# A hybrid RWKV-7, Mamba-2 and MoE block: order of the triangular inverses, place of the b and k transposes, rows of the rest weights

## The chip, the cores and the metric

One core of a Trainium2 chip runs the whole kernel in one launch. The metric is the device time in microseconds. Engines: TensorE (PE), VectorE (DVE), ScalarE (ACT), GpSimd (POOL), and SyncE (SP), which issues most of the transfers.

## The reference

One layer on 512 latent and 256 context tokens, D = 1024: adaLN modulation, a mixer of two branches (RWKV-7 in both directions, Mamba-2 SSD in both directions), a gated merge, then 16 expert-choice experts. The change touches the RWKV branch alone. Its preparation and its recurrence for each of 16 heads and both directions are:

```python
w_raw = rw_w0 + einsum('blde,def->bldf', tanh(xw), rw_w2)   # low-rank, 64 columns per direction
decay = exp(-exp(-softplus(-w_raw) - 0.5))
a = sigmoid(rw_a0 + einsum('blde,def->bldf', xa, rw_a2))
kk = l2norm(k * rw_kk);  k_eff = k * (1 + (a - 1) * rw_ka)
sa = einsum('bhvk,bhk->bhv', s, -kk_t)
s = s * w_t + sa * (kk_t * a_t) + v_t * k_t
y = einsum('bhvk,bhk->bhv', s, r_t)
```

## The kernel before

The kernel has stages: norms and adaLN (to about 110 us), the RWKV pair stage (about 110 to 690), the RWKV chunk scan (about 680 to 870), the SSD scan, the merge and the experts. The recurrence is computed in chunks of 64 tokens, 12 per direction; within a chunk the products of the scaled vectors form triangular matrices, whose inverses the scan needs.

`rw_all` runs the pair stage: eight pairs of heads, p = 0 to 7, direction d = 0 and 1 in each. Per pair: `rw_elem(p, 1)` prepares the other direction's vectors (two calls of `low()`, each two matmuls for 512 latent and two for 256 context tokens: one with `lwh`, the rounded weights, on 128 rows, and one with `lwl`, the rest weights, on the direction's 64 rows); `rw_products(p, 0)`; the bonus (`rw_bonus`); `rw_head` and `rw_elem(p + 1, 0)` for the next pair; `rw_products(p, 1)`; and `tri(p)`.

`rw_products` stores AR, multiplies BK by AR in three groups (tile `pab`, with `TENSOR_TENSOR` into X by DVE after each), stores X to DRAM, and then transposes BK in three groups of four chunks (`pbt`, copied to BT by ACT and stored to BTd by ACT's queue). A call f() after each piece pushes about 2600 columns of the input projection (`pl`, `pc`) into PE's order as fill; in the last pairs, when all inputs are projected, 1500.

`tri(p)` inverts the 16x16 and 32x32 blocks of the stored products on DVE, step by step. It loads them as Ad (three transfers), works on T, on the scratch tile W and on Tf, ends with the copy Tt<-Tf and stores Tf and Tt to DRAM. `tri2(p)` loads them back (TT in four transfers, T11 in two, A21 in two), and makes two small products on PE, `px` and `py` (32x32), and stores TT for the scan. `tri2(p - 2)` is a generator t2 that `rw_products` steps: once after each of two X tiles' stores, once after each of three `pbt` groups. tri(7) and the last two tri2 run in `rw_last`, beside the scan.

PE's order is the order in which the code is written. DVE, ACT, POOL and SP run in an order that a scheduler works out when the kernel is built, from the order written and its own estimates. Each engine then runs its instructions in order. The PSUM pool `ra` has four buffers of one tag, shared by `low()`, `pab`, `pbt`, `px`, `py`, `pvt` and `pb`.

Of the kernel before, what the change touches and what calls it, by code (L numbers as in the profile page):

```python
# [42 lines left out]
TL = 7  # L43
# [28 lines left out]
RHT = 1500  # L72
# [15 lines left out]
class Block:  # L88
# [276 lines left out]
    def setup1(self, pool, tp):  # L365
# [14 lines left out]
        nc.vector.memset(self.smask.rearrange("p (c t) -> p c t", t=64)[:, :, 0:1], 0.0)  # L380
        self.T = T = tp.tile([96, 2, 16, 16], F32, name="T")
# [175 lines left out]
    def rw_all(self, pool, ps, z):  # L557

        self.fill, self.credit = self.rw_in(pool, z), 0
        next(self.fill)  # L560
        hop = R0
        f = lambda x=1: self.feed(x * (hop if len(self.kvr) < 8 else RHT))
        self.pair = {}
        self.drain(0)
        self.rw_head(pool, ps, 0, f)
        op = self.rw_elem(pool, ps, 0, 0, f)
        t2 = iter(())
        for p in range(8):
            nxt = self.rw_elem(pool, ps, p, 1, f)
            if p > 1:  # L570
                t2 = self.tri2(self.tp, ps, "ra", p - 2)
            hop = RHOP
            self.rw_products(pool, ps, p, 0, *op, f, t2)
            op = nxt
            if p < 7:
                self.drain(p + 1)
            self.rw_bonus(pool, ps, p)
            if p < 7:
                self.rw_head(pool, ps, p + 1, f)
                nxt = self.rw_elem(pool, ps, p + 1, 0, f)  # L580
            self.rw_products(pool, ps, p, 1, *op, f, t2, p == 7)
            op = nxt
            if p < TL:
                self.finish(self.tri(self.tp, p))
        self.feed(1 << 30)

    def rw_last(self, ps):

        if TL < 7:
            yield from self.tri(self.tp, 6)  # L590
        yield from self.tri2(self.tp, ps, "A", 6)
        yield from self.tri(self.tp, 7)
        yield from self.tri2(self.tp, ps, "A", 7)
# [4 lines left out]
    def rw_head(self, pool, ps, p, f):  # L598
# [11 lines left out]
        lwl = pool.tile([128, 2, 128], F32R, name="lwl", tag="lw", bufs=1)  # L610
        nc.scalar.activation(lwh, raw, AF.Copy)
        for d, h in enumerate(H):
            nc.vector.tensor_sub(lwl[h], raw[h, :, d], lwh[h, :, d].bitcast(F32))
# [27 lines left out]
    def rw_elem(self, pool, ps, p, d, f):  # L641
# [8 lines left out]
        def low(i, bias):  # L650
            o = tile(TOK, "sa"[i], 1 + i)
            h = slice(64 * d, 64 * d + 64)
            pl, pc = self.two(ps)
            x = self.low[i, d]
            for q, c in ((pl, slice(CTX, TOK)), (pc, slice(0, CTX))):
                nc.tensor.matmul(q, lwh[:, i, d], x[:, c], start=True, stop=False)
                nc.tensor.matmul(q, lwl[h, i], x[h, c], start=False, stop=True)
                f(.5)
# [58 lines left out]
    def rw_products(self, pool, ps, p, d, AR, BK, f, t2, last=False):  # L717
# [11 lines left out]
        for u0, m in ((0, 1), (4, 2), (8, 2)):  # L729
# [13 lines left out]
            f()  # L743
        for a, X in enumerate(Xs):
# [8 lines left out]
            next(t2, None)  # L753
        if last:
            self.first = self.scan_first()

        for g in range(3):
            pt = ps.tile([128, 4, 128], F32, name="pbt", tag="ra")
            for u in range(4):
                nc.tensor.transpose(pt[:, u], BK[:, chunk(4 * g + u)].rearrange("p x t -> p (x t)"), self.ident)  # L760
            BT = pool.tile([128, 4, 128], F32, name="BT", tag="BT", bufs=2)
            nc.scalar.activation(BT, pt, AF.Copy)
            nc.scalar.dma_start(self.BTd[p // 2][2 * g:2 * g + 2, p % 2, :, d].rearrange("g k u c -> k g (u c)"),
                                BT.rearrange("k (g u) c -> k g (u c)", u=2))
            f()
            next(t2, None)

    def tri(self, pool, p):
# [19 lines left out]
        U = Tt.rearrange("p a b -> p (a b)")[:, 0:256].rearrange("p (s x) -> p s x", x=16)  # L788
# [3 lines left out]
        W = pool.tile([96, 16, 16], F32, name="W", tag="W", bufs=1)  # L792
# [1313 lines left out]
```

## Time and profile before

| | us |
|---|---|
| three runs | 2207.89, 2210.12, 2210.43 |
| median | 2210.12 |
| profiled execution | 2214.4 |
| its span | 2212.3 |

| engine | busy us | share of the span |
|---|---|---|
| PE | 1929.1 | 87% |
| PE weight loads | 1276.1 | 58% |
| DVE | 1176.1 | 53% |
| ACT | 846.7 | 38% |
| POOL | 631.3 | 29% |

The shares are means over all stages. The pair stage, about 580 us of the span, has to be read from its own stretches, waits and timelines. The largest queue of transfers, q1 (SP's), takes 64.2% of 16 DMA engines' span.

### The profile page before, as it was taken

The numbers are of one execution on the slowest core, as the hardware profiler recorded it, in microseconds if no ns is written. First come the engines' busy times: TensorE is split into PE (matmuls) and PEld (weight loads), VectorE is DVE, ScalarE is ACT, GpSimd is POOL, SyncE is SP. The second block draws the span as 40 slices with busy tenths as digits, with TensorE's granted clock in tenths as the row PEclk, the third lists the DMA queues.
The fourth block names the chain that finished last, engine by engine and source line by source line (L and its number), as shares of the span: only waits on it lengthen the run. The fifth ranks groups of instructions, "written<-read, shape, count | busy, mean of one in ns | idle before, by whom it ended". The sixth has DMA issues, their size and how long they took to land. (4 is left out here: it accounts for less than half of the span.)

```text
span 2212.3 us, 35294 instructions
## 1 busy us (share of the span) xinstructions
PE 1929.1 (87%) x13996; PEld 1276.1 (58%) x14016; DVE 1176.1 (53%) x1939; ACT 846.7 (38%) x1422; POOL 631.3 (29%) x484
## 2 busy tenths in 40 slices
PE   4979888798868857999997999789999998999997
PEld 2756666566646645666675666457888453433332
DVE  4355987887894829444443466674355112322214
ACT  5444554555443323343445345444334222111113
POOL 2244342523242222232333475664211000000002
PEclk8989988989988989999999999899999998999999
DMA  6246668767889686977555344336857898999997
GB/s 233 74 116 145 164 158 192 151 173 158 193 180 240 187 170 185 292 253 218 164 157 175 99 152 140 106 133 209 300 201 274 333 366 317 409 409 409 409 409 301
DMA packets 444655, 495.15 MB, mean 224 GB/s; under 512 B 138441, under 2 KB 339391, under 8 KB 441419
## 3 DMA queue, kind: packets, MB, share of 16 engines
q1 hardware_dynamic: 419755, 449.27, 64.2%
q0 software_dynamic: 7872, 26.75, 4.2%
q10 hardware_dynamic: 16864, 16.88, 2.4%
q8 instruction: 110, 1.80, 0.3%
q14 instruction: 54, 0.44, 0.1%
HBM read 393.95 MB, written 97.98 MB: 222 GB/s over the span
## 5 line engine op out<-in xcount | busy, mean ns | idle before, releaser
L287 POOL TENSOR_TENSOR wlo<-wraw,whi 128x1024 fp32r<-128x1024 f32 x92 | 231.4, 2515 | 505.1 <-ACT whi L284 205.9
L312 PE MATMUL pl<-hlH,whi 128*128 128x512 f32 x672 | 242.2, 438 | 17.8 <-DVE hlH L257 5.9
L312 PE MATMUL pl<-hlH,wlo 128*128 128x512 f32 x672 | 239.8, 435 | 0.0
L312 PE MATMUL pl<-hlL,whi 128*128 128x512 f32 x672 | 233.7, 428 | 0.0
L1703 PE MATMUL ph<-ew,xe 128*64 128x512 f32 x432 | 196.0, 596 | 0.8 <-DMA ew<-in_exp_w_dram 0.8
L1702 PE MATMUL ph<-ew,xe 128*64 128x512 f32 x432 | 195.5, 596 | 0.0
L284 ACT ACTIVATE whi<-wraw 128x1024 fp32r<-128x1024 f32 x93 | 98.1, 1055 | 243.7 <-DMA wraw<-in_w_in_dram 160.4
L312 PEld LDWEIGHTS pl<-hlH,whi 128*128 128x128 f32 x672 | 130.0, 198 | 61.5 <-issue 15.5
L312 PEld LDWEIGHTS pl<-hlH,wlo 128*128 128x128 f32 x672 | 129.0, 198 | 38.9 <-issue 14.1
L312 PEld LDWEIGHTS pl<-hlL,whi 128*128 128x128 f32 x672 | 127.6, 195 | 39.9 <-issue 14.2
L1702 PEld LDWEIGHTS ph<-ew,xe 128*64 128x64 f32 x432 | 56.5, 137 | 109.0 <-issue 107.5
L463 DVE SCALAR_TENSOR_TENSOR cacc<-u,cst,cacc 128x772 f32<-128x772 f32 (+1 forms) x96 | 98.4, 1025 | 33.3 <-ACT cacc L459 31.7
L315 PE MATMUL pc<-hcH,whi 128*128 128x256 f32 (+1 forms) x312 | 97.1, 312 | 20.0 <-ACT u L454 14.6
L1789 PE MATMUL pye<-ew,ewx 128*64 128x512 f32 x448 | 109.9, 642 | 0.0
L315 PE MATMUL pc<-hcL,whi 128*128 128x256 f32 (+1 forms) x312 | 95.9, 311 | 0.0
L315 PE MATMUL pc<-hcH,wlo 128*128 128x256 f32 (+1 forms) x312 | 94.9, 307 | 0.0
L1212 ACT ACTIVATE M<-sel,ncumT 128x128 f32<-128x128 f32 x256 | 69.3, 387 | 67.0 <-PE sel L1209 66.9
L1709 ACT ACTIVATE ewx<-ph 128x512 f32<-128x512 f32 x30 | 17.9, 598 | 184.3 <-PE ph L1703 171.6
L1817 DVE TENSOR_TENSOR macc<-macc,psc 128x512 f32<-128x512 f32 x56 | 37.7, 685 | 89.9 <-PE psc L1812 89.8
L1213 DVE TENSOR_TENSOR M<-M,cb 128x512 f32<-128x512 f32 x64 | 63.4, 999 | 35.0 <-ACT M L1212 34.8
L466 POOL TENSOR_TENSOR cacc<-cacc,csg 128x772 f32<-128x772 f32 (+1 forms) x24 | 42.4, 1765 | 135.2 <-ACT csg L465 134.6
L315 PEld LDWEIGHTS pc<-hcH,whi 128*128 128x128 f32 (+1 forms) x312 | 61.6, 197 | 30.2 <-ACT u L454 17.8
(574 smaller groups left out, 4228.2 us busy)
## 6 DMA issues: line engine op xcount, KB each, us to landing
ew<-in_exp_w_dram SPq DMA_DIRECT2D x126, 1024.0 KB, 16.6
ew<-in_exp_w_dram SPq DMA_DIRECT2D x90, 512.0 KB, 13.1
wraw<-in_w_in_dram SPq DMA_DIRECT2D x83, 512.0 KB, 4.1
adaw<-in_ada_w_dram SPq DMA_DIRECT2D x24, 1024.0 KB, 13.7
cst<-in_exp_w_dram SPq DMA_DIRECT2D x14, 1024.0 KB, 18.0
BTd<-BT ACTq DMA_DIRECT2D x48, 256.0 KB, 4.0
sAL<-ALd SPq DMA_DIRECT2D x23, 512.0 KB, 3.8
sBT<-BTd SPq DMA_DIRECT2D x23, 512.0 KB, 6.2
```

The lines of the kernel that those rows point to most:

```text
L284: pin(nc.scalar.activation(hi, raw, AF.Copy))
L287: self.lo.tensor_sub(lo, raw, hi.bitcast(F32))
L312: nc.tensor.matmul(pl[:n], w_[:, kt, :n], x[0][:, kt, :], **e)
L315: nc.tensor.matmul(pc[:n], w_[:, kt, :n], x[1][:, kt, :], **e)
L463: e.scalar_tensor_tensor(acc[:, s0:s0 + n0], u[:, s0 + k:s0 + k + n0], cw[:, b, k:k + 1], acc[:, s0:s0 + n0], op0=OP.mult, op1=OP.add)
L466: nc.gpsimd.tensor_mul(acc[:, s:s + n], acc[:, s:s + n], sg[:, s:s + n])
L1212: nc.scalar.activation(M[:, c], pt[:, c * 128:c * 128 + 128], AF.Exp, bias=self.ncumT[:, c, r:r + 1])
L1213: nc.vector.tensor_mul(M.rearrange("p c t -> p (c t)"), M.rearrange("p c t -> p (c t)"), cb)
L1702: nc.tensor.matmul(ph[e][f][0:64], x, w1[j][:, fs], start=kt == 0, stop=kt == 7, skip_group_check=True)
L1703: nc.tensor.matmul(ph[e][f][64:128], x, w3[j][:, fs], start=kt == 0, stop=kt == 7, skip_group_check=True)
L1789: nc.tensor.matmul(py[64 * c:64 * c + 64], hd[e][:, kt], w2[j][:, 512 * c:512 * c + 512], start=kt == 0, stop=kt == 7, skip_group_check=True)
L1817: nc.vector.tensor_add(a, a, pc)
```

## The change

1. The inverses. `TL` goes, and with it the whole `tri(p)` at the end of pair p. In pair p the generator `tr` = tri(p - 1) is stepped once by every call of f(), from `rw_elem(p, 1)` on; what is left is finished at the start of the next pair. It has 16 steps, and a pair from there has 19 calls up to the end of `rw_elem(p + 1, 0)`. tri(6) runs in pair 7.
2. `tri2(p - 2)` is started before `rw_elem(p, 1)` (its loads are written there), and stepped once in each of the three groups of `rw_products`.
3. Each of the three `pab` groups is followed by f(), f(), the `pbt` transposes of the same four chunks, their BT copy and store, f() and one step of t2. The X stores follow after all three.
4. `lwl` is one tile of 128 rows for both directions, zeroed once; each direction's 64 rows are written in their place, and the matmul takes all 128 rows.
5. W takes columns 256 to 511 of Tt's tile instead of a tile of its own.

```diff
@@ -40,7 +40,6 @@
 R0 = 3000
 SF = 2000
 HE = 0, 1
-TL = 7
 SS = 3
 RA = 0
 PL = (0, 1, -1, -2, 2, 3, 4, 5, 6, 7)
@@ -378,6 +377,8 @@
         self.smask = pool.tile([128, TOK], BF, name="smask")
         nc.gpsimd.memset(self.smask, 1.0)
         nc.vector.memset(self.smask.rearrange("p (c t) -> p c t", t=64)[:, :, 0:1], 0.0)
+        self.lwl = pool.tile([128, 2, 2, 128], F32R, name="lwl")
+        nc.vector.memset(self.lwl.bitcast(F32), 0.0)
         self.T = T = tp.tile([96, 2, 16, 16], F32, name="T")
         nc.gpsimd.memset(T, 0.0)
         for h in range(2):
@@ -559,16 +560,24 @@
         self.fill, self.credit = self.rw_in(pool, z), 0
         next(self.fill)
         hop = R0
-        f = lambda x=1: self.feed(x * (hop if len(self.kvr) < 8 else RHT))
+        tr = iter(())
+
+        def f(x=1):
+            self.feed(x * (hop if len(self.kvr) < 8 else RHT))
+            next(tr, None)
         self.pair = {}
         self.drain(0)
         self.rw_head(pool, ps, 0, f)
         op = self.rw_elem(pool, ps, 0, 0, f)
         t2 = iter(())
         for p in range(8):
-            nxt = self.rw_elem(pool, ps, p, 1, f)
+            self.finish(tr)
+            if p > 0:
+                tr = self.tri(self.tp, p - 1)
             if p > 1:
                 t2 = self.tri2(self.tp, ps, "ra", p - 2)
+                next(t2)
+            nxt = self.rw_elem(pool, ps, p, 1, f)
             hop = RHOP
             self.rw_products(pool, ps, p, 0, *op, f, t2)
             op = nxt
@@ -580,14 +589,11 @@
                 nxt = self.rw_elem(pool, ps, p + 1, 0, f)
             self.rw_products(pool, ps, p, 1, *op, f, t2, p == 7)
             op = nxt
-            if p < TL:
-                self.finish(self.tri(self.tp, p))
+        self.finish(tr)
         self.feed(1 << 30)
 
     def rw_last(self, ps):
 
-        if TL < 7:
-            yield from self.tri(self.tp, 6)
         yield from self.tri2(self.tp, ps, "A", 6)
         yield from self.tri(self.tp, 7)
         yield from self.tri2(self.tp, ps, "A", 7)
@@ -607,10 +613,10 @@
             for h in H:
                 nc.sync.dma_start(raw[h, i], self.A[n][0][:, :, p * 128:(p + 1) * 128].rearrange("d e f -> e d f"))
         lwh = pool.tile([128, 2, 2, 128], F32R, name="lwh", tag="lwh", bufs=1)
-        lwl = pool.tile([128, 2, 128], F32R, name="lwl", tag="lw", bufs=1)
+        lwl = self.lwl
         nc.scalar.activation(lwh, raw, AF.Copy)
         for d, h in enumerate(H):
-            nc.vector.tensor_sub(lwl[h], raw[h, :, d], lwh[h, :, d].bitcast(F32))
+            nc.vector.tensor_sub(lwl[h, :, d], raw[h, :, d], lwh[h, :, d].bitcast(F32))
         lw = lwh, lwl
         nkk = rn = sq = tile(TOK, "nkk")
         nc.scalar.activation(sq, k, AF.Square, scale=P["kk"][:, p:p + 1])
@@ -649,12 +655,11 @@
 
         def low(i, bias):
             o = tile(TOK, "sa"[i], 1 + i)
-            h = slice(64 * d, 64 * d + 64)
             pl, pc = self.two(ps)
             x = self.low[i, d]
             for q, c in ((pl, slice(CTX, TOK)), (pc, slice(0, CTX))):
                 nc.tensor.matmul(q, lwh[:, i, d], x[:, c], start=True, stop=False)
-                nc.tensor.matmul(q, lwl[h, i], x[h, c], start=False, stop=True)
+                nc.tensor.matmul(q, lwl[:, i, d], x[:, c], start=False, stop=True)
                 f(.5)
 
             nc.scalar.activation(o[:, CTX:], pl, AF.Tanh, bias=bias, scale=0.5)
@@ -726,7 +731,8 @@
             nc.sync.dma_start(ALd[:, H[d], d, a].rearrange("g k t -> k g t"), al[H[a], 0:6])
             nc.sync.dma_start(RTd[:, H[d], a].rearrange("g k t -> k g t"), al[H[a], 6:10])
         Xs = [pool.tile([128, 20, 64], F32, name="X", tag="X", bufs=2) for _ in range(2)]
-        for u0, m in ((0, 1), (4, 2), (8, 2)):
+        for g, m in enumerate((1, 2, 2)):
+            u0 = 4 * g
             pa = [ps.tile([128, 4, m, 64], F32, name="pab", tag="ra") for _ in range(2)]
             for u in range(4):
                 for a in range(2):
@@ -741,6 +747,16 @@
                 nc.vector.tensor_mul(o, pa[a], self.mk[:, d, None, 0:m].to_broadcast([128, 4, m, 64]))
             f()
             f()
+
+            pt = ps.tile([128, 4, 128], F32, name="pbt", tag="ra")
+            for u in range(4):
+                nc.tensor.transpose(pt[:, u], BK[:, chunk(u0 + u)].rearrange("p x t -> p (x t)"), self.ident)
+            BT = pool.tile([128, 4, 128], F32, name="BT", tag="BT", bufs=2)
+            nc.scalar.activation(BT, pt, AF.Copy)
+            nc.scalar.dma_start(self.BTd[p // 2][2 * g:2 * g + 2, p % 2, :, d].rearrange("g k u c -> k g (u c)"),
+                                BT.rearrange("k (g u) c -> k g (u c)", u=2))
+            f()
+            next(t2, None)
         for a, X in enumerate(Xs):
             xs = X.rearrange("q (g u) t -> q g (u t)", u=2)
             for b in range(2):
@@ -750,20 +766,8 @@
             nc.sync.dma_start(self.d3[p % 3][d, :, 12 * a:12 * a + 12], X[64 * d:64 * d + 32, 0:12, 32:64])
             nc.sync.dma_start(ALd[:, V[d], d, a].rearrange("g k t -> k g t"), xs[V[d], 0:6])
             nc.sync.dma_start(RBd[:, :, d, a].rearrange("g k t -> k g t"), xs[:, 6:10])
-            next(t2, None)
         if last:
             self.first = self.scan_first()
-
-        for g in range(3):
-            pt = ps.tile([128, 4, 128], F32, name="pbt", tag="ra")
-            for u in range(4):
-                nc.tensor.transpose(pt[:, u], BK[:, chunk(4 * g + u)].rearrange("p x t -> p (x t)"), self.ident)
-            BT = pool.tile([128, 4, 128], F32, name="BT", tag="BT", bufs=2)
-            nc.scalar.activation(BT, pt, AF.Copy)
-            nc.scalar.dma_start(self.BTd[p // 2][2 * g:2 * g + 2, p % 2, :, d].rearrange("g k u c -> k g (u c)"),
-                                BT.rearrange("k (g u) c -> k g (u c)", u=2))
-            f()
-            next(t2, None)
 
     def tri(self, pool, p):
 
@@ -785,11 +789,10 @@
             if s % 2 == 0:
                 yield
         Tt = pool.tile([96, 32, 32], F32, name="Tt", tag="Tt", bufs=1)
-        U = Tt.rearrange("p a b -> p (a b)")[:, 0:256].rearrange("p (s x) -> p s x", x=16)
+        U, W = (Tt.rearrange("p a b -> p (a b)")[:, i:i + 256].rearrange("p (s x) -> p s x", x=16) for i in (0, 256))
         nc.scalar.activation(U, T[:, 0].rearrange("p x s -> p s x"), AF.Copy)
         nc.scalar.activation(Tf[:, 0:16, 0:16], T[:, 0], AF.Copy)
         nc.scalar.activation(Tf[:, 16:32, 16:32], T[:, 1], AF.Copy)
-        W = pool.tile([96, 16, 16], F32, name="W", tag="W", bufs=1)
         for c in range(0, 16, 2):
             n = c + 2
             prv = prod(32 * n).rearrange("p (c s t) -> p c s t", c=2, s=16)
```

How the build orders this is shown at three places. The first is pair 5, where the loads of `tri2(3)` are issued by SP: T is T11, d_214 the stored Tf and Tt, d_211 the products that Ad reads. Before:

```order
L811 DMA d_214<-Tt 96x1024
L748 DMA d_211<-X 32x12x32 x2
L750 DMA d_216<-X 32x12x32
L751 DMA ALd_156<-X 64x6x128
L752 DMA RBd_164<-X 128x4x128
L281 DMA wraw<-in_w_in_dram 128x8x128
L825 DMA T_4784<-d_214 32x24x32
L822 DMA TT<-d_214 32x24x32 x2
L778 DMA Ad<-d_211 96x16x16 x3
L822 DMA TT<-d_214 32x24x32
L825 DMA T_4784<-d_214 32x24x32
L822 DMA TT<-d_214 32x24x32
```

and with the change:

```order
L764 DMA d_211<-X 32x12x32 x2
L766 DMA d_216<-X 32x12x32
L767 DMA ALd_156<-X 64x6x128
L768 DMA RBd_164<-X 128x4x128
L825 DMA TT<-d_214 32x24x32
L828 DMA T_4506<-d_214 32x24x32
L825 DMA TT<-d_214 32x24x32 x2
L828 DMA T_4506<-d_214 32x24x32
L825 DMA TT<-d_214 32x24x32
L782 DMA Ad<-d_211 96x16x16 x3
L731 DMA ALd_156<-AR 64x6x128
L280 DMA wraw<-in_w_in_dram 128x8x128
```

All six loads of `tri2` now stand ahead of the three Ad loads, and no wraw stands before them. In the same place on PE, `px` stood after the third `pab` group's fill, with the first transposes behind it:

```order
L315 MATMUL pc<-hcL,whi 128x256
L312 MATMUL pl<-hlL,whi 128x512
L315 MATMUL pc<-hcL,whi 128x256
L312 MATMUL pl<-hlL,whi 128x512
L836 MATMUL px<-T_4784,A_4783 32x32 x48
L760 MATMUL pbt<-ident,BK 128x128 x4
L315 MATMUL pc<-hcL,whi 128x256
L312 MATMUL pl<-hlH,wlo 128x512
L315 MATMUL pc<-hcH,wlo 128x256
L312 MATMUL pl<-hlH,wlo 128x512
```

and with the change it stands between the first group's transposes and the second `pab` group:

```order
L314 MATMUL pc<-hcH,whi 128x256
L753 MATMUL pbt<-ident,BK 128x128 x4
L311 MATMUL pl<-hlH,whi 128x512
L314 MATMUL pc<-hcH,whi 128x256
L311 MATMUL pl<-hlH,whi 128x512
L314 MATMUL pc<-hcH,whi 128x256
L311 MATMUL pl<-hlH,whi 128x512
L314 MATMUL pc<-hcH,whi 128x256
L311 MATMUL pl<-hlH,whi 128x512
L839 MATMUL px<-T_4506,A_4505 32x32 x48
L741 MATMUL pab<-AR,BK 128x128 x8
L314 MATMUL pc<-hcH,whi 128x256
```

The second place is DVE in the same pair, where tri begins with the multiply of 2 elements (96x2). Before, it stood behind X of the second group and BK:

```order
L695 SCALAR_TENSOR_TENSOR BK<-t_4665,IE 128x12x64
L329 SCALAR_TENSOR_TENSOR k<-pl,cst,k 128x511
L329 SCALAR_TENSOR_TENSOR k<-pc,cst,k 128x255
L741 TENSOR_TENSOR X<-pab,cst 128x4x2x64 x2
L699 TENSOR_TENSOR BK<-t_4669,IE 128x12x64
L783 TENSOR_TENSOR pr<-T,Ad 96x2
L741 TENSOR_TENSOR X<-pab,cst 128x4x2x64
L784 TENSOR_REDUCE T<-pr 96x2
L741 TENSOR_TENSOR X<-pab,cst 128x4x2x64
```

and with the change it stands ahead of both:

```order
L700 SCALAR_TENSOR_TENSOR BK<-t_4587,IE 128x12x64
L787 TENSOR_TENSOR pr<-T,Ad 96x2
L788 TENSOR_REDUCE T<-pr 96x2
L787 TENSOR_TENSOR pr<-T,Ad 96x8
L788 TENSOR_REDUCE T<-pr 96x2x2
L787 TENSOR_TENSOR pr<-T,Ad 96x18
L747 TENSOR_TENSOR X<-pab,cst 128x4x2x64
L788 TENSOR_REDUCE T<-pr 96x2x3
L747 TENSOR_TENSOR X<-pab,cst 128x4x2x64
L787 TENSOR_TENSOR pr<-T,Ad 96x32
L704 TENSOR_TENSOR BK<-t_4591,IE 128x12x64
```

The third place is DVE in pair 7 around the end of an inverse, Tt<-Tf. Before, BK, X, zg and ksum stood ahead of it:

```order
L695 SCALAR_TENSOR_TENSOR BK<-t_6107,IE 128x12x64
L741 TENSOR_TENSOR X<-pab,cst 128x4x2x64
L481 SCALAR_TENSOR_TENSOR zg<-zg,pl 128x8x64
L741 TENSOR_TENSOR X<-pab,cst 128x4x2x64
L804 TENSOR_TENSOR pr<-W,Tt 96x128
L804 TENSOR_TENSOR pr<-W,Tt 96x64
L741 TENSOR_TENSOR X<-pab,cst 128x4x2x64 x2
L699 TENSOR_TENSOR BK<-t_6111,IE 128x12x64
L806 TENSOR_REDUCE Tf<-pr 96x16x2 x2
L711 SCALAR_TENSOR_TENSOR ksum<-ksum,cst,r 128x512
L783 TENSOR_TENSOR pr<-T,Ad 96x2
L809 COPY Tt<-Tf 96x32x32
```

and with the change the AR multiplies, BK, X and zg stand behind it:

```order
L809 TENSOR_REDUCE Tf<-pr 96x16x2
L677 SCALAR_TENSOR_TENSOR s<-smask,s 128x768
L809 TENSOR_REDUCE Tf<-pr 96x16x2
L747 TENSOR_TENSOR X<-pab,cst 128x256
L812 COPY Tt<-Tf 96x32x32
L693 TENSOR_TENSOR AR<-nkk,E 128x256
L694 TENSOR_TENSOR AR<-nkk,E 128x512
L695 TENSOR_TENSOR AR<-r,E 128x8x64
L700 SCALAR_TENSOR_TENSOR BK<-t_6025,IE 128x12x64
L747 TENSOR_TENSOR X<-pab,cst 128x256
L482 SCALAR_TENSOR_TENSOR zg<-zg,pl 128x8x64
```

## Rows read from the trace of the kernel before

**Rows 1.** PE's waits, 130 to 880 us: line, releaser, total us, times, longest.

```profile
PE px L836 <- DMA T<-d: 30.8, 5, 12.0
PE pbt L760 <- DVE X L741: 22.5, 12, 3.3
```

**Rows 2.** Busy us by engine (x instructions), PE's granted clock, DMA share, GB/s.

```profile
165.00:220.00 55.00, 50.26 (x328) 37.03 (x327) 30.32 (x43) 26.95 (x37) 20.98 (x15) 1.00 0.63 149
...
605.00:660.00 55.00, 35.09 (x315) 24.32 (x314) 52.96 (x100) 24.53 (x36) 22.12 (x15) 0.85 0.82 179
```

**Rows 3.** PE's timeline, pair 5: start us, duration, instruction, idle before.

```profile
495.06 0.69 PE L738 MATMUL pab<-AR,BK 64*64 64x64 f32 x32
...
506.33 0.21 PE L836 MATMUL px<-T,A 32*32 32x32 f32 x2 [0.83 <-DMA T<-d]
512.46 2.74 PE L836 MATMUL px<-T,A 32*32 32x32 f32 x94 [5.91 <-DMA T<-d]
```

**Rows 4.** DVE's timeline, pairs 4 to 5, same columns.

```profile
492.27 1.08 DVE L809 COPY Tt<-Tf 96x1024 f32<-96x1024 f32 x1
...
510.01 0.41 DVE L783 TENSOR_TENSOR pr<-T,Ad 96x2 f32<-96x2 f32 x1 [3.16 <-DMA Ad<-d]
...
525.75 0.75 DVE L328 SCALAR_TENSOR_TENSOR v<-pl,cst,v 128x511 f32<-128x511 f32 x1 [3.65 <-ACT v L327]
...
527.88 0.55 DVE L783 TENSOR_TENSOR pr<-T,Ad 96x392 f32<-96x392 f32 x1
...
565.97 1.10 DVE L809 COPY Tt<-Tf 96x1024 f32<-96x1024 f32 x1
```

**Rows 5.** SP's timeline, pair 5: start us, issue time, transfer.

```profile
498.43 1.03 SPq L825 DMA_DIRECT2D T<-d  x1
...
504.67 2.57 SPq L778 DMA_DIRECT2D Ad<-d  x3
...
508.51 0.52 SPq L825 DMA_DIRECT2D T<-d  x1
```

**Rows 6.** PE's timeline around low() calls.

```profile
487.95 0.50 PE L656 MATMUL ra<-low,lwh 128*128 128x512 f32 x1 [1.58 <-DVE X L741]
488.39 0.50 PE L657 MATMUL ra<-low,lwl 64*128 64x512 f32 x1
488.82 0.39 PE L315 MATMUL pc<-hcL,whi 128*128 128x256 f32 x1
489.04 0.40 PE L312 MATMUL pl<-hlL,whi 128*128 128x512 f32 x1
489.28 0.28 PE L315 MATMUL pc<-hcL,whi 128*128 128x256 f32 x1
489.40 0.28 PE L656 MATMUL rac<-low,lwh 128*128 128x256 f32 x1
...
489.91 0.50 PE L312 MATMUL pl<-hlL,whi 128*128 128x512 f32 x1
```

**Rows 7.** PE's groups by line, 150 to 880 us: busy us, mean ns.

```profile
L657 PE MATMUL ra<-low,lwl 64*128 64x512 f32 x28 | 15.1, 540 | 0.0
...
L656 PE MATMUL ra<-low,lwh 128*128 128x512 f32 x28 | 12.8, 458 | 10.0 <-ACT VT L622 7.7 <-DVE X L741 2.3
```

**Rows 8.** Busy times and granted clock in the stretch after px.

```profile
512.50:519.40 6.90, 6.90 (x191) 6.39 (x193) 4.57 (x19) 3.16 (x6) 0.00 (x0) 0.63 0.88 203
```

**Rows 9.** PE's timeline, pairs 1 and 2.

```profile
224.55 0.66 PE L760 MATMUL pbt<-ident,BK 128*128 128x128 f32 x4 [2.34 <-DVE X L741]
...
289.00 1.71 PE L836 MATMUL px<-T,A 32*32 32x32 f32 x96
```

**Rows 10.** PE's timeline, pair 7.

```profile
656.89 3.02 PE L836 MATMUL px<-T,A 32*32 32x32 f32 x96 [12.04 <-DMA T<-d]
```

**Rows 11.** DVE's timeline, pair 7.

```profile
638.24 0.41 DVE L688 TENSOR_TENSOR AR<-nkk,E 128x256 f32<-128x256 f32 x1
...
648.07 1.02 DVE L809 COPY Tt<-Tf 96x1024 f32<-96x1024 f32 x1
```

## The prediction

> **What bounds the kernel now.** I read the list of PE's waits first, then the busy times in stretches of 55 us, then the timelines of PE, DVE and SP around one of the waits. PE is what the span is made of, so a change is worth what it takes from PE's work where PE never waits, or from the chain that ends PE's longest wait where it does. In the RWKV pair stage that is `px` (line 836), the first product of `tri2`, which waits for the inverse's tile T11 to be loaded: 30.8 us in five waits. Next comes `pbt` (line 760), which waits for a PSUM buffer that DVE still has to empty into X: 22.5 us in twelve [rows 1]. The stretches show the two ends of the stage [rows 2]: from 165 to 220 us PE is busy 50.26 of 55 us and DVE 30.32, so the first pairs are bound by PE; from 605 to 660, in the last pair, DVE is busy 52.96 us and PE 35.09.
>
> Between them the pairs run in a ring, and pairs 4 to 5 show it. On DVE the inverse ends with the copy Tt<-Tf at 492.27; `px` starts in earnest at 512.46, that is 20.2 us later [rows 3, 4]. PE then works through fill until the next pair's v projection is evacuated by DVE at 525.75, 13.3 us after `px`; and from there DVE needs 40.2 us to the next Tt<-Tf at 565.97 [rows 4]. 20.2 + 13.3 + 40.2 = 73.7 us, one pair. What lies outside the ring is hidden: a microsecond less on PE elsewhere in pairs 3 to 6 only lengthens the `px` wait.
>
> The first leg is mostly SP. After the stores and the X transfers of one product it issues the first T11 load at 498.43, then two TT loads, the three Ad loads at 504.67 (2.57 us, for the next inverse), and only at 508.51 the second T11 load, which lands at about 512.4, where `px` resumes [rows 3, 5].
>
> **The change, part by part.** The sum is made against the profiled execution: span 2212.3 us and 2.1 us around it, 2214.4 us, which is 4.3 above the median of 2210.1.
>
> *Weights padded to 128 rows.* Per `low()` call the four matmuls are the same four, but the two with `lwl` have 128 rows, half of them zero. Two sizes can be read. The mean of a 512-column matmul is 540 ns with `lwl` and 458 with `lwh` [rows 7]; that 82 ns is all a busy time shows. The pitch shows more: the `lwh` and `lwl` matmuls begin 0.44 and 0.43 us before their successor (487.95, 488.39, 488.82), where a 128-row matmul of the fill takes 0.24 for 512 columns and 0.12 for 256 (489.04, 489.28, 489.40); the 256-column pair takes 0.51 (489.40 to 489.91) [rows 6]. A call takes 0.87 + 0.51 = 1.38 us where four such 128-row matmuls take 0.72: 0.66 us too much. I take the pitch, since it is what PE's queue loses, and it holds the neighbours' loss too. The bounds are 0.08 and 0.66 us a call. There are 32 calls, but only those in the PE-bound pairs count, four in each of pairs 0 and 1 and two in pair 2's first direction: ten, at most 6.6. I take **-6**, since a little of it falls into waits that these pairs have (-0.8 to -6.6). In pairs 3 to 6 the calls lie outside the leg from `px` to v and feed the wait: nothing. The one memset of 128x512 lies on DVE in the set-up, where DVE is not the bound: nothing; uncovered it would cost about as much as the copy Tt<-Tf of 1024 elements, 1.1 us [rows 4].
>
> The 64-row matmul is the slower of the two in these rows. The Trainium skill, page "TensorE: Matmul & The Clock Gate", section "Why this matters for your kernels", says that a lone small-K matmul takes as long as a full one; by that rule padding gives nothing and the forecast would be 6 us higher (rival 3). The page "TensorEngine Tiling (Array Packing)", section "Key Properties", says that a change of tiling mode drains TensorE, which is the side on which the trace stands.
>
> *Inverses stepped through the next pair.* The generator is only asked earlier or later; the instructions stay the same. In the planned order the inverse's first multiply moves ahead of X of group 2 and of BK, and about 2.2 us more of its work stands before v (two reduces and two multiplies of 338 to 450 elements; the multiply of 392 takes 0.55 [rows 4]). The end Tt<-Tf keeps its place before the next `s`, though behind X of group 3, which PE now delivers some 3 us later. So the v leg becomes 40.2 - 2.2 = 38.0 us.
>
> *Loads.* `tri2`'s six loads now all stand ahead of the Ad loads and of the weight load wraw. SP's block up to the last T11 is shorter by Ad (2.57) and by a part of wraw: I take 2.9, and the leg becomes 20.2 - 2.9 = 17.3 us. What pays is Ad. The loads that stood between Ad's end (507.24) and 509.03, the second T11's end, and one more TT now stand ahead of it, about 2.4 us, so it lands near 512.4 where the multiply that waits for it began at 510.01 [rows 4, 5]. Behind that multiply now stand X of group 2 and BK on DVE, and PE waits for X.
>
> *`px` moved up.* Before, `px` stood behind all three product groups: PE reached it at 505.5, 10.4 us after the first group (495.06) [rows 3]. Now it comes after group 1 (0.69), ten pairs of fill matmuls of 0.36 and four transposes (0.6), 4.9 us: 5.5 us of PE work moves behind it, and so ahead of v: 13.3 + 5.5 = 18.8 us. The ring is 17.3 + 38.0 + 18.8 = 74.1 against 73.7. `px` still waits, some 9 us, only earlier in the row. Four pairs (3 to 6) at +0.4: 1.6, less the better clock of fewer short stalls, **+1**. Bounds per pair: -2 (v is not yet late when PE gets there) and +1.5 (X of group 3 holds up Tt): -8 to +6. The clock after the stall stays as it was: 0.63 of 2.4 GHz in the 6.9 us after 512.5 [rows 8], so PE is at 1.2 GHz in most of it, with the same length of work there.
>
> *Pair 2.* Its `px` ran at 289.00 without a wait [rows 9]. Whether its loads had landed 5.5 us before that no row shows; its wait can be anything from nothing to 5.5 us, less what comes back in the ring later: **+2** (0 to +4).
>
> *Transposes with each group.* Twelve transposes per product stay twelve; 48 BT copies and stores on ACT only change place. But the tag `ra` has four PSUM buffers: with a `pbt` between, the second tile of a product group takes a buffer that X must have emptied three calls of f earlier, where it was four. A call is 2600 columns, about 1.2 us. Where DVE is late that is 0.9 us per group less slack; against that, `pbt` no longer follows three groups in a row. First pairs, four products: **+1**. Bounds: of their four `pbt` waits, the longest 2.34 us [rows 9], half goes (-4), or two groups in each of four products lose 0.9 us (+7). Later pairs: hidden in the `px` wait.
>
> *Last pair.* Tt<-Tf at 648.07 and `px` at 656.89, after a wait of 12.04 us [rows 10, 11]. In the new order the work that stood between the AR multiply at 638.24 and Tt<-Tf moves behind it, all but 1.5 us of the inverse's own: 9.8 - 1.5 = 8.3 us. So T is stored near 640 and `px` could run at 640 + 8.8 = 648.6; but 5.9 us of PE work follows it that came before. 8.3 - 5.9 = 2.4, with a little for the shorter stall: **-3** (-8 to 0, as DVE is nearly full there and has the same work).
>
> Sum: -6 + 1 + 2 + 1 - 3 = -5 us: 2209.4 against the profiled 2214.4, which against the median of 2210.1 is **2205 us**. All low bounds together give -27, all high ones +16.
>
> **The rivals.** *1, the wait goes away* (2163 us): the loads land before PE needs T, and the five `px` waits (30.8 us) fall, with the work after four of them at full clock (6.9 x 0.37 = 2.6 us each) and the -6: -47. For it: the loads do come earlier. Against it: `px` comes earlier too, by more, and the ring has no shorter leg. *2, slower* (2222 us): Ad, now behind six loads, sets when X of group 2 is emptied. If v is ready before the inverse's part ahead of it is done, the 2.4 us of later Ad enters the ring in full: 4 x 2.4 = +10; with the ring of PSUM buffers at its bound of +7 and +1 for pair 2, against -6, this is +12. It decides where Ad lands past about 512 in a pair like the one shown: v comes at 512.46 - 2.9 + 18.8 = 528.4, and the DVE work from that multiply to v, 525.75 - 510.01 less the 3.65 us it idles before v, plus the 2.2 us and X and BK (2 us), is 16.3 us, 528.7 from 512.4 [rows 4]. That is close, so it has weight. *3, the padding does nothing* (2211 us): the pitch belongs to a switch of weights that stays, and the rest, +1, nearly cancels.
>
> **How the numbers follow.** Forecast 0.60, rival 1 0.07, rival 2 0.20, rival 3 0.13. The likeliest time is 2205. Within the forecast 2183 (all low bounds) to 2226 (all high ones, which hardly come together); rival 2 at 2222 lies near its upper end and half of it is held: range 2183 to 2222. 0.2%, 4.4 us, is about what this measurement can tell from no change, so the forecast lies just beyond it: of its 0.60, 0.39 faster, 0.17 same, 0.04 slower. With rival 1 (faster), rival 2 (0.18 slower, 0.02 same) and rival 3 (0.10 same, 0.03 slower): faster 0.46, same 0.29, slower 0.25.
>
> **What would show it.** Padding: the pitch of `lwl` matmuls falls to 0.24 and 0.12. `px`: waits of about 9 us in pairs 3 to 6, a new one in pair 2, and a distance of about 74 us between two Tt<-Tf copies; if it is over 75.5, with DVE waiting for Ad ahead of X, rival 2 holds; if the `px` line leaves the list of waits, rival 1. Last pair: `px` near 649. The prediction is wrong if the time goes to a place that the change does not touch, or if the pair distance moves by more than 2 us.

## The result, and the profile after

The changed kernel takes 2217.0 us (median of six runs, 2212.5 to 2220.6), the kernel before, measured beside it and again, 2206.2 (six runs, 2196.2 to 2210.4): ratio 1.0057, interval 1.0031 to 1.0083. It is slower by some 11 us where 5 us less was forecast.

The span of its profiled execution is 2210.3 us, shorter than the 2212.3 of the trace before. Both traces are one run each out of a spread of some 10 us and more, so a stage has to be compared over several traces. Three traces of the kernel before (the one shown and two more, e13 and e14) and two of the changed kernel (this one and e1) stand here; the marks are the last `py` matmul of a pair and the last transposes of the pair stage (start times, us).

| | last py of pair 2 | pair 2 to pair 6 | pair 6 to the last transposes | sum |
|---|---|---|---|---|
| before | 293.9, 292.9, 290.5 | 297.9, 295.2, 292.7 | 87.7, 85.3, 87.6 | 679.5, 673.4, 670.8 |
| changed | 291.8, 293.2 | 298.1, 301.0 | 94.5, 94.2 | 684.4, 688.4 |
| mean change | +0.1 | +4.3 | +7.5 | +11.8 |

What comes after, which the change does not touch, took 1515 to 1527 us from the last transposes to PE's last instruction in these traces, in no order by kernel. So by these traces the whole loss lies in the pair stage, and nearly two thirds of it in the last pair. The last pair is clear of the spread (85.3 to 87.7 us against 94.2 and 94.5); the +4.3 of pairs 2 to 6 is less sure, since the three traces before differ by 5.2 us there.

PE's waits from 130 to 880 us in the changed kernel (total, times, longest), against [rows 1]:

```profile
PE px L839 <- issue: 31.9, 5, 12.2
PE pab L741 <- DVE X L747: 26.4, 11, 4.3
PE rac L638 <- ACT VT L628: 18.0, 6, 3.7
...
PE px L839 <- DMA T<-d: 14.4, 7, 6.0
```

and two more lines of the kernel before, which belong to the comparison:

```profile
PE ra L656 <- ACT VT L622: 7.7, 5, 2.7
PE pab L735 <- DVE X L741: 7.4, 3, 4.2
```

`px` waits 46.3 us where it waited 30.8, in the two lines together; the line without a releaser ("issue") stands before the first two `px` matmuls, which start 4.6 us after the first T11 load is issued in the pair shown below, so I take it for the wait for that load. The wait for X has moved from `pbt` to the `pab` groups but has not grown: all of PE's waits for X come to 32.2, 30.0 and 31.7 us in the three traces before and to 29.2 and 33.0 in the two of the changed kernel. The wait for the VT copy, now at `rac` in `rw_head`, has doubled, from 8.4 to 10.4 us before (`ra` and `rac` together) to 18.0 and 19.4.

PE's timeline in pair 5, against [rows 3]:

```profile
492.54 0.69 PE L744 MATMUL pab<-AR,BK 64*64 64x64 f32 x32
...
503.05 0.28 PE L839 MATMUL px<-T,A 32*32 32x32 f32 x2 [5.69 <-issue]
505.18 2.73 PE L839 MATMUL px<-T,A 32*32 32x32 f32 x94 [1.85 <-DMA T<-d]
507.84 2.08 PE L741 MATMUL pab<-AR,BK 64*128 64x128 f32 x16
...
515.77 1.71 PE L849 MATMUL py<-TT,A 32*32 32x32 f32 x96
```

`px` now stands between the first group's fill and the second group. PE reached it at 497.4 and stood still for 5.7 and 1.9 us. On DVE and SP in the same pair, against [rows 4, 5]:

```profile
487.98 1.12 DVE L812 COPY Tt<-Tf 96x1024 f32<-96x1024 f32 x1
...
508.05 0.16 DVE L787 TENSOR_TENSOR pr<-T,Ad 96x2 f32<-96x2 f32 x1 [4.09 <-DMA Ad<-d]
...
526.28 0.74 DVE L327 SCALAR_TENSOR_TENSOR v<-pl,cst,v 128x511 f32<-128x511 f32 x1
...
562.47 1.13 DVE L812 COPY Tt<-Tf 96x1024 f32<-96x1024 f32 x1
```

```profile
498.47 0.61 SPq L828 DMA_DIRECT2D T<-d  x1
...
501.19 0.58 SPq L828 DMA_DIRECT2D T<-d  x1
...
502.63 3.35 SPq L782 DMA_DIRECT2D Ad<-d  x3
```

From Tt<-Tf to `px` 17.2 us, from there to v 21.1, from v to Tt<-Tf 36.2: 74.5 us. The second T11 load is issued ahead of Ad and lands 4.0 us after; the first multiply that needs Ad begins 20.1 us after Tt<-Tf, where it was 17.7.

In the last pair, against [rows 10, 11], first PE, then DVE:

```profile
649.39 0.28 PE L839 MATMUL px<-T,A 32*32 32x32 f32 x2 [12.22 <-issue]
650.15 2.77 PE L839 MATMUL px<-T,A 32*32 32x32 f32 x94 [0.48 <-DMA T<-d]
652.84 2.08 PE L741 MATMUL pab<-AR,BK 64*128 64x128 f32 x16
...
660.24 1.16 PE L741 MATMUL pab<-AR,BK 64*128 64x128 f32 x16
...
672.91 0.48 PE L741 MATMUL pab<-AR,BK 64*128 64x128 f32 x2 [2.95 <-DVE ksum L719]
675.24 2.07 PE L741 MATMUL pab<-AR,BK 64*128 64x128 f32 x14 [1.85 <-DVE X L747]
...
684.06 0.60 PE L753 MATMUL pbt<-ident,BK 128*128 128x128 f32 x4
```

```profile
637.71 2.17 DVE L812 COPY Tt<-Tf 96x1024 f32<-96x1024 f32 x1
...
667.73 3.41 DVE L807 TENSOR_TENSOR pr<-Tt 96x512 f32<-96x512 f32 x2
671.06 1.20 DVE L809 TENSOR_REDUCE Tf<-pr 96x32 f32<-96x512 f32 x2
672.18 0.67 DVE L719 TENSOR_TENSOR ksum<-v,pb 128x512 f32<-128x512 f32 x1
...
674.76 0.42 DVE L747 TENSOR_TENSOR X<-pab,cst 128x256 f32<-128x256 f32 x1 [1.04 <-issue]
...
680.46 1.09 DVE L812 COPY Tt<-Tf 96x1024 f32<-96x1024 f32 x1
```

The inverse ends at 637.71, ten us earlier than in [rows 11]; counted from the last `py` of pair 6, it ends 8.1 us earlier on the mean of the five traces. `px` starts at 649.39 instead of 656.89. The step from Tt<-Tf to `px` has become longer, 11.7 us where it was 8.8, and SP shows why. First the changed kernel, then the kernel before:

```profile
637.77 0.61 SPq L813 DMA_DIRECT2D d<-Tf  x1
638.49 0.99 SPq L782 DMA_DIRECT2D Ad<-d  x1
...
641.13 2.71 SPq L782 DMA_DIRECT2D Ad<-d  x2
643.94 1.62 SPq L731 DMA_DIRECT2D ALd<-AR  x1
645.65 1.45 SPq L828 DMA_DIRECT2D T<-d  x2
```

```profile
647.75 0.52 SPq L810 DMA_DIRECT2D d<-Tf  x1
...
653.13 1.81 SPq L825 DMA_DIRECT2D T<-d  x2
```

In the last pair the three Ad loads of the next inverse and a store of AR stand ahead of the T11 loads, the other way round from pair 5. The T11 loads are issued 7.9 us after Tt<-Tf (7.8 in e1), where they were issued 5.1, 4.8 and 5.2 us after it before.

The last transpose begins 35.0 us after `px`, where it was 22.6. Two groups of products and their X had been done ahead of `px`; now they stand behind it, and PE waits there on DVE: 1.2 us at the third group of the first product, then 2.95 and 1.85 as shown, 6.0 in all. Before, PE waited there for 0.2 us at most in any of the three traces. In the DVE lines the multiplies and reduces of the next inverse (667.73 to 672.18) stand ahead of ksum, which empties the bonus's PSUM buffer and releases the first of the two waits, and of the X at 674.76, which releases the second. That inverse ends at 680.46, as it did before (680.1).

### The profile page after: what moved, and what is told of

The parts are those of the page before. It is cut to its first block, busy times and chain, and to the rows that moved or that the text cites. A ratio compares the mean times of both kernels' runs of the same rounds, so it can differ in the third digit from the quotient of the medians.

```text
span 2210.3 us, 35295 instructions
## 1 busy us (share of the span) xinstructions
PE 1905.5 (86%) x13996; PEld 1286.3 (58%) x14016; DVE 1172.7 (53%) x1940; ACT 844.1 (38%) x1422; POOL 632.9 (29%) x484
## 5 line engine op out<-in xcount | busy, mean ns | idle before, releaser
L311 PE MATMUL pl<-hlH,whi 128*128 128x512 f32 x672 | 249.3, 447 | 17.7 <-DVE hlH L256 5.9
L311 PE MATMUL pl<-hlH,wlo 128*128 128x512 f32 x672 | 230.4, 422 | 0.0
L314 PE MATMUL pc<-hcL,whi 128*128 128x256 f32 (+1 forms) x312 | 94.5, 306 | 0.0
L1215 ACT ACTIVATE M<-sel,ncumT 128x128 f32<-128x128 f32 x256 | 69.2, 386 | 62.1 <-PE sel L1212 62.0
L314 PEld LDWEIGHTS pc<-hcH,whi 128*128 128x128 f32 (+1 forms) x312 | 65.4, 209 | 30.8 <-ACT u L455 16.9
```

Source lines behind the costliest of these rows:

```text
L311: nc.tensor.matmul(pl[:n], w_[:, kt, :n], x[0][:, kt, :], **e)
L314: nc.tensor.matmul(pc[:n], w_[:, kt, :n], x[1][:, kt, :], **e)
L1215: nc.scalar.activation(M[:, c], pt[:, c * 128:c * 128 + 128], AF.Exp, bias=self.ncumT[:, c, r:r + 1])
```

## The experiments

Ratios are against the kernel before, on the same chip, with 95% intervals. e1 to e4, e5 to e8, e9 to e12 and e13 to e15 ran on four different chips, so versions of different groups are compared by their ratios. The edits show the telling lines; "..." marks lines left out.

**e1: the changed kernel again.** No edit.

> The changed kernel itself, once more, on one chip with the runs of the kernel before. Theory A (the loss is real and lies in the pair stage): ratio 1.004 to 1.007, and the pair stage to the first px of the chunk scan ends 8 us or more later than in a run of the kernel before from the same chip. Theory B (the difference is a level of the chip or of the expert stage, which the change does not touch): ratio within 0.998 to 1.002.

Measured 1.0065 (1.0048 to 1.0081), 2219.5 us. The loss is there in a second set of runs, and the pair stage ends at 688.4, against 670.8 to 679.5 in the traces of the kernel before. Theory A holds.

**e2, e3, e4: one part alone.** e2 is the kernel before with the padded weights (and W in Tt's tile); e3 with the stepped inverses; e4 with the transposes in the groups and `tri2` started early.

```diff
 e2
+        self.lwl = pool.tile([128, 2, 2, 128], F32R, name="lwl")
...
-                nc.tensor.matmul(q, lwl[h, i], x[h, c], start=False, stop=True)
+                nc.tensor.matmul(q, lwl[:, i, d], x[:, c], start=False, stop=True)
 e3
+            next(tr, None)
...
+                tr = self.tri(self.tp, p - 1)
...
-            if p < TL:
-                self.finish(self.tri(self.tp, p))
 e4
+                next(t2)
...
+            pt = ps.tile([128, 4, 128], F32, name="pbt", tag="ra")
...
+            f()
+            next(t2, None)
```

> The kernel before with the rest weights padded to 128 rows alone (and W in Tt's tile, which makes room). By the prediction's pitch: 6 us faster, ratio 0.997. By its rival 3: 1.000. If padding is what costs: over 1.002.

> The kernel before with the inverses stepped through the next pair alone; transposes, tri2's steps and weights as before. If the loss comes from where the inverse stands on DVE: over 1.003. By the prediction: within 0.998 to 1.001, with the gain of some 3 us in the last pair.

> The kernel before with the transposes moved into the product groups and tri2 started early and stepped once per group, alone; inverses and weights as before. If the loss comes from px standing earlier on PE (it waits longer and has 5.5 us more work between it and v) or from the PSUM ring: 1.004 to 1.008. By the prediction's sum: 1.001 to 1.002.

Measured: e2 0.9993 (0.9979 to 1.0006), e3 0.9996 (0.9981 to 1.0011), e4 1.0085 (1.0066 to 1.0104). Padding and stepping are worth nothing that can be measured alone; e2's time is the one that rival 3 named, though in its trace the pitches do fall to 0.23 and 0.12 us. The loss comes with the third part, which holds three things: the place of `px`, the place of the transposes, and the early loads. In e4's trace the Tt<-Tf copies are 54.6, 91.9, 65.6, 88.9 and 70.7 us apart, short and long by turns, so what is read above from single pairs of the changed kernel does not carry over to it.

**e5, e6, e9: the place of px.** The changed kernel, with `px` and `py` moved: in e5 in the last pair alone and in e6 in every pair, `px` comes after the third group's transposes and `py` after the call of f() behind them; in e9, in every pair, `px` after the second group and `py` after the third.

```diff
 e6 (e5: late = p == 7)
+            late = True
+            if late and g == 2:
+                next(t2, None)
             f()
-            next(t2, None)
+            if not late or g == 2:
+                next(t2, None)
 e9
-            next(t2, None)
+            if g:
+                next(t2, None)
```

> The changed kernel, but in the last pair alone px runs after the third product group's transposes and py after the fill behind them; all else as changed. Theory Tail (in the last pair two more product groups stand behind the px wait, with X of them on DVE; the stretch from py to the last transposes grew from 14.5 to 24.2 us): 6 to 8 us faster than the changed kernel, ratio 1.002 to 1.004. Rival (the loss lies in pairs 2 to 6): 1.006, as the changed kernel.

> The changed kernel with px after the third product group in every pair; transposes stay within the groups, loads stay early. If the place of px on PE is the whole loss: 0.998 to 1.001. If a part comes from the transposes within the groups (X stored later, PSUM buffers): 1.002 to 1.004 and no better than px late in the last pair alone.

> The changed kernel with px after the second product group in every pair and py after the third: half way between the changed kernel (after the first: 1.0065) and px after the third (0.9928). If each group of PE work (some 4.5 us) that stands behind px lengthens the ring and the tail in proportion: 0.999 to 1.001. If there is a threshold, the loads' 17 us, that PE's work ahead of px has to cover: near 1.005 or near 0.994.

Measured: e5 1.0033 (1.0016 to 1.0050), e9 1.0040 (1.0023 to 1.0057), e6 0.9928 (0.9908 to 0.9949), 2191.3 us. e5 is some 5 to 7 us faster than the changed kernel (1.0057 and 1.0065), and its trace shows where: the last pair takes 86.9 us from `py` to the last transposes, as before the change, and pairs 2 to 6 take 300.3, as with it. `px` of the last pair in e5 starts without a wait:

```profile
652.39 1.71 PE L843 MATMUL px<-T,A 32*32 32x32 f32 x96
```

e6 is some 28 us faster than the changed kernel and 14 to 16 faster than the kernel before, better than either theory had it. No proportion holds between the three places: one group later gives 4 to 6 us, with intervals that meet, two give 28. The trace of e9 does not show its loss: its pair stage ends at 672.3, no later than those of the kernel before, so where e9 loses its 0.4% stays open. In e6 PE's waits from 255 to 600 us (pairs 2 to 6) begin with these, and the one wait of `px` on a load that is left is that of the last pair:

```profile
PE pab L741 <- DVE X L747: 19.9, 12, 4.1
PE px L843 <- DVE X L747: 8.1, 4, 3.6
PE py L853 <- ACT A L846: 7.9, 8, 2.8
```

```profile
636.12 3.13 PE L843 MATMUL px<-T,A 32*32 32x32 f32 x96 [15.11 <-DMA T<-d]
```

In pair 5 of e6, PE and then DVE:

```profile
490.24 0.95 PE L843 MATMUL px<-T,A 32*32 32x32 f32 x48
494.75 1.49 PE L843 MATMUL px<-T,A 32*32 32x32 f32 x48 [3.56 <-DVE X L747]
```

```profile
473.59 1.12 DVE L816 COPY Tt<-Tf 96x1024 f32<-96x1024 f32 x1
...
502.98 0.75 DVE L327 SCALAR_TENSOR_TENSOR v<-pl,cst,v 128x511 f32<-128x511 f32 x1 [0.34 <-ACT v L326]
...
541.17 1.09 DVE L816 COPY Tt<-Tf 96x1024 f32<-96x1024 f32 x1
```

From Tt<-Tf to `px` 16.7 us, with no wait for a load; from `px` to v 12.7; from v to Tt<-Tf 38.2: 67.6 us, where the changed kernel has 74.5. Only the middle leg is shorter. It holds the PE work between `px` and v, and that work is what the place of `px` sets. PE's busy time and clock from 304 to 600 us, in a trace of the kernel before (e13), the changed kernel and e6, show PE idle for 47.7, 56.9 and 42.0 us of the 296:

```profile
304.00:600.00 296.00, 248.32 (x2160) 188.45 (x2161) 240.50 (x430) 144.32 (x212) 105.45 (x64) 0.89 0.76 171
```

```profile
304.00:600.00 296.00, 239.06 (x2157) 196.18 (x2158) 237.79 (x421) 140.88 (x208) 103.66 (x64) 0.86 0.73 168
```

```profile
304.00:600.00 296.00, 253.96 (x2271) 204.41 (x2272) 242.05 (x455) 155.54 (x234) 120.98 (x69) 0.91 0.75 177
```

**e7, e8, e15: the early loads and the transposes.** e7 is the kernel before with `tri2`'s loads written early and `px` where it was; e8 is the same with padded weights and stepped inverses, so that against e6 the transposes stand elsewhere (at the end, three groups in a row) and `px` with them: ahead of the transposes in e8, behind them and two more calls of f() in e6. e15 is e6 without the early start of `tri2`.

```diff
 e7, e8
+                next(t2)
+            nxt = self.rw_elem(pool, ps, p, 1, f)
...
-            next(t2, None)
+            if a:
+                next(t2, None)
 e15 (to e6)
-                next(t2)
...
-            if not late or g == 2:
+            if g != 1:
```

> The kernel before with tri2's loads written ahead of the other direction's vectors, alone; px and py at their old places, transposes at the end, inverses and weights as before. If Ad behind six loads costs (rival 2 of the prediction): 1.003 to 1.005. If the earlier loads shorten the leg to px with px at its old place: 0.996 to 0.999.

> Weights padded, inverses stepped, loads early, but transposes at the end and px at its old place, as before. With px late in all pairs as the only other difference, this against that one is the price of the transposes within the groups. Theory Tail and place of px: 0.997 to 1.000. Rival (loads early cost by themselves): 1.003.

> The changed kernel with px after the third group in every pair, but tri2 not started early: its loads are written after the first group. In the planned order the T11 loads still stand ahead of Ad, three of the four TT loads behind it. If the early loads carry a part of the gain: 0.995 to 0.999. If px late with transposes in the groups is all of it: 0.992 to 0.994.

Measured: e7 0.9985 (0.9970 to 1.0000), e8 0.9999 (0.9981 to 1.0017), e15 0.9967 (0.9948 to 0.9986). The early loads alone cost nothing. In e7 and e8 no wait of `px` on a load is left in pairs 3 to 6 either, and yet e8 gains nothing: four pairs take 72.7 us each there (pvt to pvt), against 70.0 in e6, with 4.2 us of `pbt` waiting for X in each. So moving the transposes into the groups is worth 14 to 16 us, with `px` behind them. e15 puts the early start's part of e6's gain at 0.4%, with intervals that meet; its pair stage ends at 668.9, 9.7 us after e6's.

**e10, e11: padding and stepping with px late.** e6 with the weights on 64 rows (e10), and with each inverse written whole at its pair's end (e11).

```diff
 e10 (to e6)
-                nc.tensor.matmul(q, lwl[:, i, d], x[:, c], start=False, stop=True)
+                nc.tensor.matmul(q, lwl[h, i], x[h, c], start=False, stop=True)
 e11 (to e6)
-            next(tr, None)
...
+            if p < 7:
+                self.finish(self.tri(self.tp, p))
```

> px after the third group in every pair, all else as changed, but the rest weights on 64 rows as before. With the px wait gone the pairs are nearer to PE's own pace, so padding should show here: by the pitch, 0.66 us for each of some 28 calls, up to 15 us, ratio 0.996 to 1.000. If padding is worth nothing: 0.993, as with it.

> px after the third group in every pair, all else as changed, but each inverse written whole at its pair's end as before. If the stepping costs or gains nothing: 0.993. If it keeps X ahead of the inverse on DVE and so matters for the transposes in the groups: 0.996 or more.

Measured: e10 0.9963 (0.9947 to 0.9978), e11 0.9993 (0.9975 to 1.0010). Against e6 the padding is worth 0.35%, some 8 us (the intervals meet), and the stepping 0.65%, some 14. Neither could be measured alone. The traces of e10 and e6 do not show the 8 us (their pair stages end at 659.8 and 659.2); that figure rests on the timed runs. The traced execution of e10 was the fastest of its eleven (2189.9 us, median 2196.1), that of e6 the slowest of its six (2192.8).

**e12: px of the last pair later still.**

```diff
 e12 (to the changed kernel)
+            if (p < 7 and g == 2) or (p == 7 and d == 1 and g == 0):
+                next(t2, None)
             f()
-            next(t2, None)
+            if (p < 7 and g == 2) or (p == 7 and d == 1 and g == 1):
+                next(t2, None)
```

> px after the third group in every pair, but in the last pair after the first group of the second product, py after its second group. The wait of 15 us before px in the last pair is the longest left. If PE's place alone sets it: 4 to 8 us faster than with px after the third group, ratio 0.989 to 0.991. If DVE, busy 51 to 53 of 55 us there, sets the last pair anyway: 0.992 to 0.993.

Measured 0.9927 (0.9906 to 0.9948), 2186.7 us, beside 0.9928 for e6. The ratio does not move, as was expected if DVE sets the last pair. The trace speaks against that reason: the last pair takes 80.0 us in it, against 88.2 in e6, and the pair stage ends at 648.9 instead of 659.2. But these are one trace each, and the timed runs do not have the 10 us, so no gain is shown and the reason stays open. e6 and e12 are the fastest versions found.

**e13, e14: the kernel before, two more profiles.** No edit.

> The kernel before, unchanged, one more profile. If the first trace was typical: four pairs from the third to the seventh pvt take 298 us (74.7 each), and the last transposes of the pair stage begin near 679. If it was a slow one: about 291 us (72.6 each), and near 671.

> The same again, for the spread between two profiles of one kernel: under 3 us between their pair stages if the ring is regular; up to 8 us if it has more than one rhythm.

The pair stage ends at 673.4 and 670.8 where the first trace had 679.5; two traces of one kernel differ by 3 us, three by 9. The first trace, from which the prediction was read, was the slowest of the three. The four pairs take 73.9 and 73.2 us each, against 74.7 in it: the same rhythm, a little shorter.

## Why the prediction was wrong

*Padded weights, -6.* The size of the pitch was nearly right. The call in [rows 6] takes 1.38 us; over the calls from 200 to 705 us the median pitches are 0.33, 0.43, 0.21 and 0.31, or 1.28 us, and with the change 0.23, 0.24, 0.12 and 0.12, or 0.71. The `lwl` matmul of the changed kernel begins 0.23 us before its successor at 512 columns, where [rows 6] had 0.43; the two matmuls of 256 columns take 0.24 (491.50 to 491.74) where they took 0.51; and the mean of 512 columns falls from 540 [rows 7] to 413 ns:

```profile
490.33 0.39 PE L661 MATMUL ra<-low,lwh 128*128 128x512 f32 x1
490.56 0.39 PE L662 MATMUL ra<-low,lwl 128*128 128x512 f32 x1
490.79 0.28 PE L314 MATMUL pc<-hcL,whi 128*128 128x256 f32 x1
...
491.50 0.28 PE L661 MATMUL rac<-low,lwh 128*128 128x256 f32 x1
491.62 0.28 PE L662 MATMUL rac<-low,lwl 128*128 128x256 f32 x1
491.74 0.28 PE L314 MATMUL pc<-hcH,wlo 128*128 128x256 f32 x1
```

```profile
L662 PE MATMUL ra<-low,lwl 128*128 128x512 f32 x28 | 11.6, 413 | 0.0
```

What failed is the step from there to the end, that in the first pairs PE's time is the end's time. The changed kernel reaches the first `pvt` of pair 2 some 3 us earlier (231.3 and 232.9, against 235.4, 235.3 and 234.3), and pair 2 gives it back: 72.7 and 73.5 us to the next pair's `pvt`, against 69.2, 69.1 and 67.6, since `px` of pair 2 now waits 6.0 us, where [rows 9] had no wait. With that and the transposes the three terms -6, +1 and +2 came to +0.1 at the last `py` of pair 2. The 8 us that e10 shows appear only with `px` late. The Trainium skill, "TensorE: Matmul & The Clock Gate", section "Why this matters for your kernels", gives a lone small-K matmul the time of a full one; the rows above go against it here, by 0.20 us at 512 columns. They agree with the page "TensorEngine Tiling (Array Packing)" of the Trainium skill, section "Key Properties", by which changing the tiling mode drains the engine; no run here shows the drain by itself.

*The ring, +1.* The legs were forecast at 17.3, 18.8 and 38.0 and came at 17.2, 21.1 and 36.2. The sum of 74.1 came at 74.5, in part by luck, as the misses of 2.3 and 1.8 nearly cancel, and the Tt<-Tf copies of the changed kernel are 73.7, 72.1, 75.2, 74.5 and 75.2 us apart. `px` waits 7.5 us in the pair shown (forecast: some 9). The waits and the leg from `px` to v went the way that was forecast, and the term is +4.3 over pairs 2 to 6 rather than +1, with the doubt of 5 us between traces said above. That this ring sets the pair was too strong, though: in e7 the wait of `px` for its load is gone from pairs 3 to 6, and the kernel is at most 0.3% faster.

*Ad, and rival 2.* Ad came 2.4 us later in the pair shown, as forecast. Rival 2's mark, over 75.5 us between two Tt<-Tf, is not reached in the trace shown; e1 has 76.3 once, but so has a trace of the kernel before (76.2 in e13), so the mark tells little. In e6 the multiply that needs Ad begins 17.4 to 18.7 us after Tt<-Tf in pairs 3 to 6, against 15.1 to 18.3 before, and the pairs are the shortest, so a late Ad does not cost by itself. Whether it has a share in the +4.3 while `px` is early, no run takes apart. Rival 2 named a time near the measured one (2222), but by luck: it put 10 us into the ring, 7 into the PSUM buffers of the first pairs and nothing into the last pair, where most of the loss is.

*The last pair, -3.* This is the step that failed most. Measured +7.5, and moving `px` and `py` of that pair alone (e5) gives 5 to 7 of it back. `px` was to come 8.3 us earlier, with 5.9 us of PE work following it that came before. The inverse did end 8.1 us earlier, but `px` came only 5.6 us earlier (59.5 us after the last `py` of pair 6, against 65.1): the 8.8 us from Tt<-Tf to `px` were carried over as they were and came at 11.7, since the T11 loads stand behind the Ad loads in this pair. And the stretch behind `px` grew by 12.4, not 5.9: I counted PE's instructions there and left out that DVE empties each of those groups into X, and the bonus into ksum, in line with the next inverse, and that PE waits for it in turn (6.0 us). The two omissions, some 3 and 6 us, make up most of the way from -3 to the measured loss; the lines show them, and e5 shows that with `px` behind the groups nearly all of that loss goes.

*Rival 1, set at 0.07.* In pairs 3 to 6 the wait of `px` does go away with the early loads, if `px` stays behind the three groups (e6, e7, e8). It is worth nothing by itself: e7 and e8 are at 0.9985 and 0.9999, where rival 1 had 47 us. I weighed the new place of `px` only for the kernel as changed, where it nearly cancels against the other legs, and so called it a small term. It is the term that decides in the kernel as changed: 28 us between the two places.

*The level.* The forecast was set against a median of 2210.1 from three runs; with more runs the kernel before stands at 2204 to 2207. Against that level the forecast would have been some 4 us lower, so the level hides a part of the miss: the two times differ by 12 us, but the change was forecast at -5 and came at +11, a miss of 16. That 2217.0 lies below the 2222 at the top of the range is no merit of the mechanism either; that end was rival 2's.

What stays open: why, with `px` late, the transposes in the groups are worth 14 to 16 us and the stepped inverses 14, where the stepping alone gives nothing, and why e9 is slower than the kernel before. The traces do not show which wait ends last in each case. It was not tried with more PSUM buffers.

## What to carry to other kernels

Where a short product waits for a loaded result in a loop, the work between it and the next thing that its chain needs is a leg of the loop: try it late on its engine, and let the load run under work that has to be done anyway; here the place behind all three groups was the best of those tried. A wait that goes away is not yet time gained (e7, e8), and parts of a change that are worth nothing alone (here padding and stepping, under 0.1% each) can be worth 0.35% and 0.65% together with the right third part. And before a forecast of a few microseconds, take two or three traces of the same kernel: here they differ by 9 us in one stage.

## What the runs showed of the hardware

A matmul with 64 rows between matmuls with 128 takes longer than the same with 128 rows, half of them zero: 0.43 us of pitch at 512 columns against 0.23. The matmul ahead of it gains too: the `lwh` matmul's pitch falls from 0.33 to 0.23 (medians). The profiled executions of one unchanged kernel spread by 11 us (2203.1 to 2214.4), with clocks of 0.936 to 0.939. The pair stage ends at times that differ by 9 us in them, and what follows it, by 10; no cause for that spread was looked for.
